# Row terms, output-weight scaling and recurrence products of the first mixer on VectorE, with alpha folded into scales

## The chip, the cores and the metric

The kernel runs on one core of a Trainium2 chip. The metric is the device time of one execution in microseconds; it is the median of three runs. Five engines work side by side, each through its own queue in order: TensorE (PE), VectorE (DVE), ScalarE (ACT), GpSimd (POOL) and SyncE (SP), which here only starts transfers.

## The reference

Two transformer blocks over 512 rows of 1024 numbers in float32. Only the first block is touched:

```python
mod = silu(c) @ w_ada + b_ada
sh_m, sc_m, gt_m, sh_f, sc_f, gt_f = split(mod, 6)        # six modulation rows
u = layer_norm(x) * (1 + sc_m) + sh_m
mix = hybrid_mixer(u, ...)
x = layer_norm(ALPHA * x + (1 + gt_m) * mix, ln1_g, ln1_b)   # ALPHA = 2 ** 0.25
u = layer_norm(x) * (1 + sc_f) + sh_f
ffn = hierarchical_moe(u, ...)                              # 16 experts
x = layer_norm(ALPHA * x + (1 + gt_f) * ffn, ln2_g, ln2_b)

# hybrid_mixer
q, k, v, f_logit, xb, gb = split(u @ w_in)
attn = forgetting_attention(q, k, v, f_logit + b_f)         # 8 heads, causal
xc = causal_conv4(xb) + conv_b                              # rg_lru_branch
a = exp(-8 * sigmoid(gate_r(xc)) * softplus(-lam))
h = scan(h = a * h + sqrt(1 - a * a) * sigmoid(gate_i(xc)) * xc)
lru = h * gelu(gb)
mix = concat(rms_norm(attn, g_attn), rms_norm(lru, g_lru)) @ w_out
```

## The kernel before

Matrix products run in three passes. A weight tile of 128x1024 is loaded (`wraw`), rounded on ScalarE into a high half (`whi`, L275), and the rest is taken on VectorE (`wlo`, L283); L522 to L524 multiply hi by hi, hi by lo and lo by hi. The first mixer fills about the first 323 us of the span. Its weights come in the fixed order xb (4 tiles), gb (4), v (4), q and k in turn (4 each), then eight tiles of the output weight `w_out`. Work for the other engines is written as tasks (generators); between two steps of the projections, each task is advanced by one `yield`. So the place of an operation in an engine's queue follows from how many yields stand before it.

Three tasks are touched. `forget` works out the forget gate. `lru_task` (L988) is the recurrent branch: for two column blocks at a time `conv` (VectorE, L917 and L920) and `gates` (two matmuls, L928, then ScalarE), and after both of them `recur`, with products on VectorE (L945 to L950), one product on GpSimd (L951), the scan on VectorE (L954) and one more product on GpSimd (L958). `ada_rest` (L1195) makes the modulation rows gt_m, sc_f, sh_f, gt_f, in this order: eight tiles of w_ada are loaded by SyncE per row, and tile k, scaled by one column of `cs`, is added to the row. For gt_m this is one VectorE instruction per tile (L1231); for the other three a scaling on ScalarE (L1234) and an add on GpSimd (L1235). `ada_rest` also multiplies the four row tiles of x by ALPHA on GpSimd (L1239).

Before `lru_task` starts, `lru_params` (L1063) works out softplus(-lam) and some halved biases from 4 columns. `times_gt` (L681) multiplies each of the eight output-weight tiles by the row gt_m, on GpSimd, ahead of its split. `mixed` squares a finished column block, adds the squares to those before on GpSimd (L974), and splits the block into halves (L975, L976); `row_scale` turns the sums into 1/rms (L453 to L461), and L1152 adds a product, times that scale, to x. In the attention, one unit's tile runs through the mask (L575), the exponential on ScalarE (L582), reciprocal and scaling (L586, L587), transposes on TensorE (L591) and a copy out of them (L614 or ScalarE's L616).

In the mixture of experts, GpSimd multiplies the four tiles of the new x by ALPHA (L1984, experts 8 to 11).

Of the kernel before, what the change touches and what calls it, by code (L numbers as in the profile page):

```python
# [18 lines left out]
D = 1024  # L19
# [9 lines left out]
RMS_EPS = 1e-6  # L29
ALPHA = 2.0 ** 0.25  # L30
HD = 64
RAWS, PARTS = 5, 4
# [344 lines left out]
class Kern:  # L377
# [303 lines left out]
    def times_gt(self, t, n):  # L681

        assert "gt_m" in self.rows_done
        gt = self.rows["gt_m"][:, None, 512 * n:512 * n + 512]
        self.nc.gpsimd.tensor_tensor(out=t, in0=t, in1=gt.to_broadcast([128, 2, 512]),
                                     op=OP.mult)
# [6 lines left out]
    def first_mixer(self):  # L693
# [10 lines left out]
        for i in range(NT):  # L704
# [11 lines left out]
                               op1=OP.mult)  # L716
        v.tensor_scalar(cs, cs, 0.5, None, op0=OP.mult)


# [178 lines left out]
        xbp, gl, xc, th, tg, ae = {}, {}, {}, {}, {}, {}  # L898
        sp2 = fb.tile([128, 4], F32, name="sp2")
        sp4 = fb.tile([128, 4], F32, name="sp4")  # L900
        brg = fb.tile([128, 4], F32, name="brg")
        big_ = fb.tile([128, 4], F32, name="big")

        def lru_params():
            self.log1p_exp_neg_abs(sp2, self.small("lam", 0, 4), 4)
            nl = self.st(4)
            v.tensor_scalar(nl, self.small("lam", 0, 4), -1.0, 0.0, op0=OP.mult, op1=OP.max)
            v.tensor_tensor(out=sp2, in0=sp2, in1=nl, op=OP.add)
            v.tensor_scalar(sp2, sp2, 2.0, None, op0=OP.mult)
            v.tensor_scalar(sp4, sp2, -2.0, None, op0=OP.mult)  # L910
            v.tensor_scalar(brg, self.small("b_rg", 0, 4), 0.5, None, op0=OP.mult)
            v.tensor_scalar(big_, self.small("b_ig", 0, 4), 0.5, None, op0=OP.mult)

        def conv(m):
# [24 lines left out]
        def recur(m):  # L939


            sq, d = self.g(), self.g()
            t, a, x_c = th.pop(m), ae.pop(m), xc.pop(m)
            nc.scalar.activation(out=sq, in_=t, func=AF.Sqrt, scale=0.25)
            v.scalar_tensor_tensor(out=t, in0=a, scalar=1.0, in1=t, op0=OP.add, op1=OP.mult)  # L945
            v.scalar_tensor_tensor(out=x_c, in0=tg.pop(m), scalar=1.0, in1=x_c,
                                   op0=OP.add, op1=OP.mult)
            yield
            v.scalar_tensor_tensor(out=sq, in0=a, scalar=1.0, in1=sq, op0=OP.add, op1=OP.mult)
            v.tensor_scalar(t, t, -1.0, 1.0, op0=OP.mult, op1=OP.add)  # L950
            nc.gpsimd.tensor_tensor(out=sq, in0=sq, in1=x_c, op=OP.mult)  # L951
            yield
            a = t
            v.tensor_tensor_scan(out=d, data0=a, data1=sq, initial=0.0, op0=OP.mult, op1=OP.add)  # L954
            del a, sq, t, x_c
            while m not in gl:
                yield
            nc.gpsimd.tensor_tensor(out=gl[m], in0=d, in1=gl[m], op=OP.mult)  # L958
            self.dump(f"lruT{m}", gl[m])
            ready.add(("lru", m))  # L960
# [5 lines left out]
        def mixed(nm, m, src, hl):  # L966

            g = self.small(nm, m)
            s2 = self.g()
            nc.scalar.activation(out=s2, in_=src, func=AF.Square)  # L970
            if m == 0:
                ssq[nm] = s2
            else:
                nc.gpsimd.tensor_tensor(out=ssq[nm], in0=ssq[nm], in1=s2, op=OP.add)  # L974
            nc.scalar.activation(out=hl[0][:, m, :], in_=src, func=AF.Copy, scale=g)  # L975
            v.scalar_tensor_tensor(out=hl[1][:, m, :], in0=src, scalar=g,  # L976
                                   in1=hl[0][:, m, :].bitcast(F32), op0=OP.mult,
                                   op1=OP.subtract)

        def row_scale(nm, out):  # L980
            ps = self.psA()
            s2 = ssq.pop(nm)
            for i in range(NT):
                nc.tensor.matmul(ps[:, i:i + 1], lhsT=s2[:, 128 * i:128 * i + 128],
                                 rhs=ones[:, 0:1], start=True, stop=True)
            self.rsqrt(out, ps[:, 0:4], 1.0 / 512, RMS_EPS, 4)

        def lru_task():  # L988
            for pair in range(2):
                for m in (2 * pair, 2 * pair + 1):  # L990
                    while m not in xbp:
                        yield
                    conv(m)
                    yield
                    yield from gates(m)
                    yield
# [65 lines left out]

        lru_params()  # L1063
        ps = self.psA()
# [130 lines left out]
    def ada_rest(self):  # L1195
# [23 lines left out]
        for q, nm in enumerate(names):  # L1219
# [4 lines left out]
            for k in range(KD + 1):  # L1224
                t, nxt = nxt, None
                if k < KD:
                    nxt = self.wp.tile([128, 1024], F32, tag="w", name="ada")
                    nc.sync.dma_start(out=nxt, in_=self.ins["w_ada"][0][
                        128 * k:128 * k + 128, cols[nm]:cols[nm] + 1024])
                if t is not None and q == 0:  # L1230
                    nc.vector.scalar_tensor_tensor(out=a, in0=t, scalar=self.cs[:, k - 1:k],  # L1231
                                                   in1=a, op0=OP.mult, op1=OP.add)
                elif t is not None:
                    nc.scalar.activation(out=t, in_=t, func=AF.Copy, scale=self.cs[:, k - 1:k])  # L1234
                    pool.tensor_tensor(out=a, in0=a, in1=t, op=OP.add)  # L1235
                del t
                if q == 0 and k in (3, 5, 6, 7):
                    i = (3, 5, 6, 7).index(k)
                    pool.tensor_scalar(self.x[:, i, :], self.x[:, i, :], ALPHA, 0.0,  # L1239
                                       op0=OP.mult, op1=OP.add)  # L1240
                yield
                if k == 5 and q > 0:
                    yield from spread(names[q - 1])
# [91 lines left out]
    def first_moe(self):  # L1335
# [25 lines left out]
        def chain(i, dep, pss, before, before_logits):  # L1361
# [54 lines left out]
            g = add("V", 1.2, times(ln1[0]), [d] + before)  # L1416
            r = self.steps_rsqrt(steps, z, q, 1.0 / D, self.eps_ln, -0.5 * LN_EPS)
            m = add("V", 0.3, mean2, [r, g])
# [427 lines left out]
        def places():  # L1846
# [5 lines left out]
            v.reciprocal(out=w1, in_=w1)  # L1852
            v.tensor_tensor(out=w1, in0=w1, in1=gw, op=OP.mult)
            v.tensor_tensor(out=w2, in0=w1, in1=e2, op=OP.mult)
# [103 lines left out]
        for e in range(NE):  # L1958
# [21 lines left out]
            if e == 6:  # L1980
                self.tasks.append(places())
            elif e in (8, 9, 10, 11):
                i = e - 8
                nc.gpsimd.tensor_scalar(x[:, i, :], x[:, i, :], ALPHA, 0.0, op0=OP.mult,  # L1984
                                        op1=OP.add)
            if W.n_dma >= W.limit or e == NE - 1:
# [76 lines left out]
        def tail(i):  # L2063
# [17 lines left out]
            def squares(q, bias):  # L2081
# [14 lines left out]
                op0=OP.add, op1=OP.mult), [d], late=late) for h in range(2)]  # L2096
            r = rsqrt(d, 1.0 / D, self.eps_ln, -0.5 * LN_EPS)
            e = add("A", 0.62, lambda: nc.scalar.activation(
# [984 lines left out]
def kernel(ctx, tc, names, *aps, dbg=None, stop=None):  # L3083
# [24 lines left out]
    k.eps_ln = base.tile([128, 1], F32, name="eps_ln")  # L3108
    nc.vector.memset(k.eps_ln, LN_EPS)
    k.st_first = ExitStack()  # L3110
    k.first = k.pool(k.st_first, "first")
# [106 lines left out]
```

## Time and profile before

| | us |
|---|---|
| median of three runs | 2336.22 (2334.93 to 2337.41) |
| the profiled execution | 2334.09, span 2332.3 |
| TensorE busy in the span | 2201.1 (94%) |
| VectorE busy | 1508.5 (65%) |
| ScalarE busy | 1175.1 (50%) |
| GpSimd busy | 462.2 (20%) |

The page gives each engine's busy time and share of the span, the span in 40 slices, the chain of work that ended last, and groups of instructions with what ended the idle time before them. A timeline lists one engine's instructions by start time, neighbours of one line together, and in brackets how long the engine stood idle before it and which instruction released it.

### The profile page before, as it was taken

Reading aid. Unit: us, or ns where it says so; the run is one execution under the profiler, and the core shown is the slowest. Engines: PE = TensorE matmul, PEld = TensorE weight load, DVE = VectorE, ACT = ScalarE, POOL = GpSimd, SP = SyncE. Lnnn points to the kernel's source line nnn. Section 1 sums busy time; section 2 is a strip of 40 time slices with the busy share of each in tenths; the row PEclk is TensorE's granted clock in tenths of the full one; section 3 lists DMA queues with packets and bytes.
Section 4 is the critical chain, followed back from the end, with each engine's and each line's share of the span. In section 5 each row is a group of like instructions: output and inputs, shape, how many; then the busy total and the mean of one; then the engine's idle time right before and its main releaser. Section 6 shows DMA issues by size and latency. Waiting matters only on the chain.

```text
span 2332.3 us, 30052 instructions
## 1 busy us (share of the span) xinstructions
PE 2201.1 (94%) x10972; PEld 1752.4 (75%) x10972; DVE 1508.5 (65%) x2552; ACT 1175.1 (50%) x2034; POOL 462.2 (20%) x377
## 2 busy tenths in 40 slices
PE   7788786998998799999999999999999999999998
PEld 4566465775565788888888888888888888888887
DVE  7845577979888866656567665257665656666623
ACT  5565444766666666554354443246654435444421
POOL 2465323445544522100000000012310000000000
PEclk9899997999999899999999999999999999999999
DMA  9453227999988433323323333223332332333321
GB/s 301 145 173 117 103 85 254 360 292 311 317 269 273 148 96 90 92 63 109 100 82 100 97 93 118 91 90 91 96 95 60 89 111 84 99 98 100 101 98 64
DMA packets 298092, 323.77 MB, mean 139 GB/s; under 512 B 10976, under 2 KB 216816, under 8 KB 297936
## 3 DMA queue, kind: packets, MB, share of 16 engines
q1 hardware_dynamic: 285904, 281.77, 38.0%
q0 software_dynamic: 12032, 40.00, 5.3%
q8 instruction: 88, 1.44, 0.3%
q14 instruction: 68, 0.56, 0.1%
HBM read 305.15 MB, written 16.52 MB: 138 GB/s over the span
## 4 chain that ended last, share of the span: by engine, by line
PE 71%; DVE 8%; ACT 3%; issue 2%; DMA 1%; POOL 1%; DVEq 0%; ACTq 0%; POOLq 0%
PE ps L523 21%; PE ps L522 21%; PE ps L524 21%; PE ps L2398 2%; DVE wlo L283 2%; PE ps L2561 1%; PE ps L591 1%; PE ps L1331 1%; ACT whi L275 1%; ACT g L2974 1%; PE ps L2680 1%; DVE st L494 1%; PE ps L1443 0%; POOL wlo L283 0%; DVE x L2953 0%
## 5 line engine op out<-in xcount | busy, mean ns | idle before, releaser
L283 DVE TENSOR_TENSOR wlo<-wraw,whi 128x1024 fp32r<-128x1024 f32 (+1 forms) x337 | 433.6, 1290 | 348.0 <-ACT whi L275 181.4
L522 PE MATMUL ps<-hT,whi 128*128 128x512 f32 x1280 | 503.7, 394 | 0.0
L524 PE MATMUL ps<-hT,wlo 128*128 128x512 f32 x1280 | 499.4, 390 | 0.0
L523 PE MATMUL ps<-hT,whi 128*128 128x512 f32 x1280 | 499.1, 390 | 0.0
L275 ACT ACTIVATE whi<-wraw 128x1024 fp32r<-128x1024 f32 (+1 forms) x346 | 360.4, 1048 | 211.4 <-DVE wlo L283 147.4
L524 PEld LDWEIGHTS ps<-hT,wlo 128*128 128x128 f32 x1280 | 240.2, 188 | 51.7
L522 PEld LDWEIGHTS ps<-hT,whi 128*128 128x128 f32 x1280 | 241.0, 188 | 47.3
L523 PEld LDWEIGHTS ps<-hT,whi 128*128 128x128 f32 x1280 | 240.5, 188 | 45.1
L522 PE MATMUL ps<-whi,hi 128*128 128x512 f32 x480 | 189.4, 394 | 0.0
L523 PE MATMUL ps<-wlo,hi 128*128 128x512 f32 x480 | 189.3, 394 | 0.0
L524 PE MATMUL ps<-whi,lo 128*128 128x512 f32 x480 | 189.3, 394 | 0.0
L523 PE MATMUL ps<-wlo,hl 128*128 128x512 f32 (+4 forms) x432 | 175.0, 405 | 9.6 <-DVE wlo L283 6.4
L522 PE MATMUL ps<-whi,hl 128*128 128x512 f32 (+4 forms) x432 | 177.1, 410 | 0.4 <-ACT hl L1638 0.4
L524 PE MATMUL ps<-whi,hl 128*128 128x512 f32 (+4 forms) x432 | 173.4, 401 | 2.6 <-DVE hl L1639 2.6
L283 DVE TENSOR_TENSOR wlo<-wx,whi 128x1024 fp32r<-128x1024 f32 x107 | 147.0, 1396 | 15.2 <-ACT whi L275 13.5
L275 ACT ACTIVATE whi<-wx 128x1024 fp32r<-128x1024 f32 x121 | 125.8, 1058 | 40.4 <-PE ps L523 27.2
L596 ACT ACTIVATE gr<-ps 128x256 fp32r<-128x256 f32 (+2 forms) x128 | 49.1, 384 | 113.8 <-PE ps L591 112.7
L524 PEld LDWEIGHTS ps<-whi,lo 128*128 128x128 f32 x480 | 90.1, 188 | 21.3
L522 PEld LDWEIGHTS ps<-whi,hi 128*128 128x128 f32 x480 | 90.2, 188 | 21.1
L523 PEld LDWEIGHTS ps<-wlo,hi 128*128 128x128 f32 x480 | 90.1, 188 | 21.0
L523 PEld LDWEIGHTS ps<-wlo,hl 128*128 128x128 f32 (+4 forms) x432 | 71.3, 165 | 45.5 <-DVE wlo L283 12.7
L3037 ACT ACTIVATE g<-ps,small 128x512 f32<-128x512 f32 x88 | 68.1, 774 | 61.7 <-PE ps L524 61.7
(506 smaller groups left out, 3994.2 us busy)
## 6 DMA issues: line engine op xcount, KB each, us to landing
wraw<-in_w_in_dram SPq DMA_DIRECT2D x108, 512.0 KB, 3.9
wraw<-in_w_up_dram SPq DMA_DIRECT2D x88, 512.0 KB, 3.8
wx<-in_w_e_down_dram SPq DMA_DIRECT2D x46, 512.0 KB, 4.5
wraw<-in_w_down_dram SPq DMA_DIRECT2D x44, 512.0 KB, 3.6
wx<-in_w_e_gate_dram SPq DMA_DIRECT2D x39, 512.0 KB, 6.3
wx<-in_w_e_up_dram SPq DMA_DIRECT2D x36, 512.0 KB, 7.0
ada<-in_w_ada_dram SPq DMA_DIRECT2D x32, 512.0 KB, 4.6
wraw<-in_w_e_up_dram SPq DMA_DIRECT2D x28, 512.0 KB, 8.4
```

Source lines behind the costliest of these rows:

```text
L275: self.k.nc.scalar.activation(out=hi[:, 0:n_el], in_=t[:, 0:n_el], func=AF.Copy)
L283: eng.tensor_tensor(out=lo[:, 0:n_el], in0=t[:, 0:n_el], in1=hi[:, 0:n_el].bitcast(F32), op=OP.subtract)
L494: p = steps.add("V", 0.13, lambda: v.scalar_tensor_tensor(out=z["q"], in0=z["y"], scalar=z["y"], in1=z["h"], op0=OP.mult, op1=OP.mult), [y ...
L522: mm(ps, lhsT=lhsT[0], rhs=rhs[0], start=first, stop=False)
L523: mm(ps, lhsT=lhsT[0], rhs=rhs[1], start=False, stop=False)
L524: mm(ps, lhsT=lhsT[1], rhs=rhs[0], start=False, stop=last)
L591: nc.tensor.transpose(pt_ps[:, c * 128:(c + 1) * 128], p[:, c * 128:(c + 1) * 128], self.const("ident"))
L596: nc.scalar.activation(out=hi, in_=pt_ps[:, 0:n], func=AF.Copy)
L1331: self.nc.tensor.transpose(pt[:, c * r:(c + 1) * r], src[:, k * 128:(k + 1) * 128], self.ident[0:r, 0:r])
L2398: self.nc.tensor.matmul(ps[q][:, c], lhsT=ws[q][w][:, k, :], rhs=act()[t][k][:, c], start=(j == 0 and k == 0), stop=(j == 2 and k == KD - 1))
L2561: nc.tensor.matmul(ps, lhsT=q, rhs=view(k[part]), start=(part == 0), stop=(part == 1))
L3037: nc.scalar.activation(out=c, in_=ps, func=AF.Identity, scale=w[1], bias=self.small("conv_b2", 44 * l + tile_))
```

## The change

1. `ada_rest`: all four rows are summed on VectorE, one instruction per tile (L1236); ScalarE's 24 scalings and GpSimd's 24 adds are gone. For gt_m a second yield stands behind each tile.
2. `times_gt` (L687), the two products of `recur` (L955, L962) and the adds of `mixed` (L978) go from GpSimd to VectorE.
3. x isn't multiplied by ALPHA any more, neither in the mixer nor in the experts. 1/ALPHA goes into the two scales of `row_scale` and into the router's weight w1 instead, and the epsilon of both normalisations behind is divided by ALPHA squared, so that they return the same.
4. `lru_params` is called at the start of the mixer, ahead of the first normalisation's statistics.
5. `lru_task` yields once more between `conv` and `gates`.

```diff
     def times_gt(self, t, n):
-        self.nc.gpsimd.tensor_tensor(out=t, in0=t, in1=gt.to_broadcast([128, 2, 512]),
+        self.nc.vector.tensor_tensor(out=t, in0=t, in1=gt.to_broadcast([128, 2, 512]),
                                      op=OP.mult)
...
+        def lru_params():
+            self.log1p_exp_neg_abs(sp2, self.small("lam", 0, 4), 4)
...
+        lru_params()
...
         def recur(m):
-            nc.gpsimd.tensor_tensor(out=sq, in0=sq, in1=x_c, op=OP.mult)
+            v.tensor_tensor(out=sq, in0=sq, in1=x_c, op=OP.mult)
...
-            nc.gpsimd.tensor_tensor(out=gl[m], in0=d, in1=gl[m], op=OP.mult)
+            v.tensor_tensor(out=gl[m], in0=d, in1=gl[m], op=OP.mult)
...
-                nc.gpsimd.tensor_tensor(out=ssq[nm], in0=ssq[nm], in1=s2, op=OP.add)
+                v.tensor_tensor(out=ssq[nm], in0=ssq[nm], in1=s2, op=OP.add)
...
-            self.rsqrt(out, ps[:, 0:4], 1.0 / 512, RMS_EPS, 4)
+            self.rsqrt(out, ps[:, 0:4], ALPHA * ALPHA / 512, ALPHA * ALPHA * RMS_EPS, 4)
...
                     conv(m)
                     yield
+                    yield
                     yield from gates(m)
...
-        lru_params()
         ps = self.psA()
...
-                if t is not None and q == 0:
+                if t is not None:
                     nc.vector.scalar_tensor_tensor(out=a, in0=t, scalar=self.cs[:, k - 1:k],
                                                    in1=a, op0=OP.mult, op1=OP.add)
-                elif t is not None:
-                    nc.scalar.activation(out=t, in_=t, func=AF.Copy, scale=self.cs[:, k - 1:k])
-                    pool.tensor_tensor(out=a, in0=a, in1=t, op=OP.add)
                 del t
-                if q == 0 and k in (3, 5, 6, 7):
-                    i = (3, 5, 6, 7).index(k)
-                    pool.tensor_scalar(self.x[:, i, :], self.x[:, i, :], ALPHA, 0.0,
-                                       op0=OP.mult, op1=OP.add)
                 yield
+                if q < 1:
+                    yield
...
-            v.tensor_tensor(out=w1, in0=w1, in1=gw, op=OP.mult)
+            v.scalar_tensor_tensor(out=w1, in0=w1, scalar=1.0 / ALPHA, in1=gw, op0=OP.mult,
+                                   op1=OP.mult)
...
-            elif e in (8, 9, 10, 11):
-                i = e - 8
-                nc.gpsimd.tensor_scalar(x[:, i, :], x[:, i, :], ALPHA, 0.0, op0=OP.mult,
-                                        op1=OP.add)
```

VectorE at the recurrence of the first two column blocks, before: terms of gt_m (L1231), the two products ahead of the scan (L945, L946), a split, two more (L949, L950) and the scan, which the program lists as L954.

```order
L1231 SCALAR_TENSOR_TENSOR gt_m<-ada,cs,gt_m 128x1024 x2
L283 TENSOR_TENSOR wlo<-wraw,whi 128x1024
L1231 SCALAR_TENSOR_TENSOR gt_m<-ada,cs,gt_m 128x1024
L945 SCALAR_TENSOR_TENSOR g<-g 128x512
L946 SCALAR_TENSOR_TENSOR g<-g 128x512
L283 TENSOR_TENSOR wlo<-wraw,whi 128x1024
L949 SCALAR_TENSOR_TENSOR g<-g 128x512
L950 TENSOR_SCALAR g<-g 128x512
L954 SCALAR_TENSOR_TENSOR g<-g 128x512
```

The same place now: the line numbers are shifted by 4, gt_m is L1236, the product that was GpSimd's is L955, the scan L958, and the product with the gelu L962.

```order
L1236 SCALAR_TENSOR_TENSOR gt_m<-ada,cs,gt_m 128x1024
L949 SCALAR_TENSOR_TENSOR g<-g 128x512
L950 SCALAR_TENSOR_TENSOR g<-g 128x512
L285 TENSOR_TENSOR wlo<-wraw,whi 128x1024
L953 SCALAR_TENSOR_TENSOR g<-g 128x512
L954 TENSOR_SCALAR g<-g 128x512
L955 TENSOR_TENSOR g<-g 128x512
L1236 SCALAR_TENSOR_TENSOR gt_m<-ada,cs,gt_m 128x1024
L958 SCALAR_TENSOR_TENSOR g<-g 128x512
L962 TENSOR_TENSOR g<-g 128x512
```

Between the fourth product and the scan there stand one new product and a term of the row, and behind the scan the second new product.

VectorE at the first unit of the attention, before: the last scan, three splits of q and k, then the mask (L575, two rows), reciprocal, scaling.

```order
L954 SCALAR_TENSOR_TENSOR g<-g 128x512
L283 TENSOR_TENSOR wlo<-wraw,whi 128x1024 x3
L575 ISA g,st<-ps,const 128x128
L575 ISA st 128x1
L586 RECIPROCAL st<-st 128x1
L587 TENSOR_SCALAR g<-g,st 128x128
```

The same place now:

```order
L285 TENSOR_TENSOR wlo<-wraw,whi 128x1024
L1236 SCALAR_TENSOR_TENSOR sc_f<-ada,cs,sc_f 128x1024 x3
L285 TENSOR_TENSOR wlo<-wraw,whi 128x1024
L1236 SCALAR_TENSOR_TENSOR sh_f<-ada,cs,sh_f 128x1024 x3
L577 ISA g,st<-ps,const 128x128
L577 ISA st 128x1
L1236 SCALAR_TENSOR_TENSOR sh_f<-ada,cs,sh_f 128x1024
L588 RECIPROCAL st<-st 128x1
L589 TENSOR_SCALAR g<-g,st 128x128
```

Six terms of sc_f and sh_f stand between the last recurrence and the first mask, and a seventh behind the mask, ahead of the reciprocal.

VectorE at the output weights, before: scaling and mask of one unit, two splits, and the first operation of a `row_scale`.

```order
L587 TENSOR_SCALAR g<-g,st 128x384
L575 ISA g,st<-ps,const 128x384
L575 ISA st 128x1
L283 TENSOR_TENSOR wlo<-wraw,whi 128x1024 x2
L453 TENSOR_SCALAR st<-ps 128x4
```

The same place now:

```order
L589 TENSOR_SCALAR g<-g,st 128x384
L577 ISA g,st<-ps,const 128x384
L577 ISA st 128x1
L687 TENSOR_TENSOR wraw<-wraw,gt_m 128x1024
L285 TENSOR_TENSOR wlo<-wraw,whi 128x1024
L687 TENSOR_TENSOR wraw<-wraw,gt_m 128x1024
L285 TENSOR_TENSOR wlo<-wraw,whi 128x1024
L455 TENSOR_SCALAR st<-ps 128x4
```

Each split has the product with gt_m in front of it; three more of these products stand further behind, between the adds to x and the reciprocal of the next unit.

## Rows read from the trace of the kernel before

**Rows 1.** Page: busy time by engine, then the chain that ended last.

```profile
PE 2201.1 (94%) x10972; PEld 1752.4 (75%) x10972; DVE 1508.5 (65%) x2552; ACT 1175.1 (50%) x2034; POOL 462.2 (20%) x377
...
PE 71%; DVE 8%; ACT 3%; issue 2%; DMA 1%; POOL 1%; DVEq 0%; ACTq 0%; POOLq 0%
```

**Rows 2.** What TensorE waited for, 36 to 325 us: total, times, longest.

```profile
PE ps L928 <- DVE g L920: 11.9, 2, 9.1
...
PE ps L591 <- DVE g L587: 6.5, 3, 5.0
...
PE ps L624 <- DVE g L614: 2.9, 2, 1.8
...
PE ps L885 <- issue: 0.9, 1, 0.9
...
PE ps L522 <- DVE st L575: 0.2, 1, 0.2
```

**Rows 3.** TensorE's timeline: start, us, engine, line, operation, [idle before <- releaser].

```profile
74.29 2.84 PE L928 MATMUL ps<-g,bd 128*128 128x512 f32 x4 [2.86 <-DVE g L920]
...
106.72 3.78 PE L928 MATMUL ps<-g,bd 128*128 128x512 f32 x4 [9.09 <-DVE g L920]
...
145.00 0.79 PE L524 MATMUL ps<-uT,wlo 128*128 128x512 f32 x1 [4.29 <-DVE wlo L283]
...
172.68 0.47 PE L591 MATMUL ps<-ident,g 128*128 128x128 f32 x1 [4.95 <-DVE g L587]
...
289.47 2.07 PE L1013 MATMUL ps<-ka,qa 68*128 68x512 f32 x2 [7.72 <-DVE st L453]
```

**Rows 4.** Stretches: busy us of PE, PEld, DVE, ACT, POOL; clock, DMA share, GB/s.

```profile
74.00:172.00 98.00, 80.06 (x302) 60.33 (x302) 55.58 (x46) 59.51 (x70) 52.40 (x25) 0.89 0.48 149
...
108.00:110.00 2.00, 2.00 (x4) 0.73 (x3) 1.94 (x1) 0.69 (x1) 0.86 (x1) 0.50 0.75 220
...
180.00:245.00 65.00, 58.73 (x274) 39.81 (x274) 33.42 (x85) 31.78 (x70) 30.91 (x17) 0.95 0.28 97
```

**Rows 5.** VectorE's timeline, 82 to 148 us.

```profile
82.53 0.69 DVE L946 SCALAR_TENSOR_TENSOR g<-g 128x512 f32<-128x512 f32 x1
83.13 1.22 DVE L283 TENSOR_TENSOR wlo<-wraw,whi 128x1024 fp32r<-128x1024 f32 x1
...
92.12 3.43 DVE L283 TENSOR_TENSOR wlo<-wraw,whi 128x1024 fp32r<-128x1024 f32 x1
...
97.67 3.35 DVE L954 TENSOR_TENSOR_SCAN g<-g 128x512 f32<-128x512 f32 x1 [1.18 <-POOL g L951]
...
147.06 1.23 DVE L954 TENSOR_TENSOR_SCAN g<-g 128x512 f32<-128x512 f32 x1 [1.18 <-POOL g L951]
```

**Rows 6.** GpSimd's timeline at 91 us.

```profile
91.60 2.86 POOL L1235 TENSOR_TENSOR sc_f<-sc_f,ada 128x1024 f32<-128x1024 f32 x1
```

**Rows 7.** VectorE's timeline, 45 to 51 us.

```profile
45.73 0.17 DVE L509 TENSOR_SCALAR g<-g 128x4 f32<-128x4 f32 x1 [0.30 <-ACT g L508]
...
49.84 1.28 DVE L1231 SCALAR_TENSOR_TENSOR gt_m<-ada,cs,gt_m 128x1024 f32<-128x1024 f32 x1
...
51.04 1.22 DVE L283 TENSOR_TENSOR wlo<-wraw,whi 128x1024 fp32r<-128x1024 f32 x1
```

**Rows 8.** Everything that touches the row tiles named ada: waits until a load, landing.

```profile
  DMA ada<-in_w_ada_dram: 16.3, 5
...
DMA to landing us min/median/max: 3.5/4.6/10.0
```

**Rows 9.** VectorE's timeline, 280 to 297 us.

```profile
282.67 6.68 DVE L283 TENSOR_TENSOR wlo<-wraw,whi 128x1024 fp32r<-128x1024 f32 x2 [1.72 <-ACT whi L275]
...
295.94 0.49 DVE L587 TENSOR_SCALAR g<-g,st 128x512 f32<-128x512 f32 x1
```

**Rows 10.** GpSimd's timeline at 583 us.

```profile
583.65 2.85 POOL L1984 TENSOR_SCALAR x<-x 128x1024 f32<-128x1024 f32 x1
```

**Rows 11.** TensorE's timeline at 589 us.

```profile
589.83 0.46 PE L523 MATMUL ps<-wlo,hl 128*80 128x512 f32 x1 [1.98 <-POOL wlo L283]
```

More of the change, by code (lines that the diff above doesn't have):

```diff
@@ L30 @@
 ALPHA = 2.0 ** 0.25
+LN_EPS2 = LN_EPS / ALPHA ** 2
 HD = 64
@@ L717, in first_mixer @@
         v.tensor_scalar(cs, cs, 0.5, None, op0=OP.mult)
+        sp2 = fb.tile([128, 4], F32, name="sp2")
+        sp4 = fb.tile([128, 4], F32, name="sp4")
+        brg = fb.tile([128, 4], F32, name="brg")
+        big_ = fb.tile([128, 4], F32, name="big")
+        def lru_params():
+            self.log1p_exp_neg_abs(sp2, self.small("lam", 0, 4), 4)
+            nl = self.st(4)
+            v.tensor_scalar(nl, self.small("lam", 0, 4), -1.0, 0.0, op0=OP.mult, op1=OP.max)
+            v.tensor_tensor(out=sp2, in0=sp2, in1=nl, op=OP.add)
+            v.tensor_scalar(sp2, sp2, 2.0, None, op0=OP.mult)
+            v.tensor_scalar(sp4, sp2, -2.0, None, op0=OP.mult)
+            v.tensor_scalar(brg, self.small("b_rg", 0, 4), 0.5, None, op0=OP.mult)
+            v.tensor_scalar(big_, self.small("b_ig", 0, 4), 0.5, None, op0=OP.mult)
+        lru_params()
         xnT = [t.rearrange("p (a b) -> p a b", a=2) for t in self.row_tiles(["xnT"] * 4)]
@@ L898, in first_mixer @@
         xbp, gl, xc, th, tg, ae = {}, {}, {}, {}, {}, {}
[L899 to L912, printed above, removed]
         def conv(m):
@@ L1416, in chain @@
             g = add("V", 1.2, times(ln1[0]), [d] + before)
-            r = self.steps_rsqrt(steps, z, q, 1.0 / D, self.eps_ln, -0.5 * LN_EPS)
+            r = self.steps_rsqrt(steps, z, q, 1.0 / D, self.eps_ln2, -0.5 * LN_EPS2)
             m = add("V", 0.3, mean2, [r, g])
@@ L2096, in tail @@
                 op0=OP.add, op1=OP.mult), [d], late=late) for h in range(2)]
-            r = rsqrt(d, 1.0 / D, self.eps_ln, -0.5 * LN_EPS)
+            r = rsqrt(d, 1.0 / D, self.eps_ln2, -0.5 * LN_EPS2)
             e = add("A", 0.62, lambda: nc.scalar.activation(
@@ L3109 @@
     nc.vector.memset(k.eps_ln, LN_EPS)
+    k.eps_ln2 = base.tile([128, 1], F32, name="eps_ln2")
+    nc.vector.memset(k.eps_ln2, LN_EPS2)
     k.st_first = ExitStack()
```

## The prediction

> **What bounds the kernel now.** I read the page first. TensorE is busy for 94% of the span, and the chain that ended last runs through it for 71% and through VectorE for 8% [rows 1]. So a microsecond matters where TensorE stands still. The view of what TensorE waited for between 36 and 325 us, the first mixer, has fourteen lines that add up to 47.3 us; most of them name VectorE [rows 2]. The timeline puts the five longest at 74.29, 106.72, 145.00, 172.68 and 289.47 us: 28.9 us in all [rows 3]. Each costs more than itself: behind the 9.09 us wait the granted clock is 0.50, and over 74 to 172 us it averages 0.89 [rows 4]. 0.11 of 98 us is 10.8 us of full-speed time, part of it in the waits themselves.
>
> Why is VectorE late? Its timeline shows one split of a weight (wlo) taking 1.22 us at 83.13 and the same shape taking 3.43 us at 92.12; one scan takes 1.23 us at 147.06 and another 3.35 us at 97.67 [rows 5]. GpSimd's add of a modulation row starts at 91.60 and takes 2.86 us, across the start of the long split [rows 6]. I read the excess as VectorE being held by a GpSimd operation with two tiles in, and by the same comparison counted about 43 us of excess in 40 to 320 us (an estimate over all VectorE rows there, normal against stretched; the splits and scans quoted are its pattern). The Trainium skill's page "SBUF — State Buffer", section "Who interferes with whom", says that a VectorE instruction with two SBUF inputs and a GpSimd instruction that reads SBUF share an interface, and that the second fully blocks. By that rule the trace agrees: 3.43 less 1.22 is 2.21 us, inside one 2.86 us add.
>
> **The change, part by part.** The sum is made against the profiled execution, 2334.09 us, which is 2.1 us under the median of 2336.22.
>
> Work that moves to VectorE: 24 row terms at 1.28 us busy [rows 7], 1.20 when queued (from the start of the term at 49.84 to that of the split behind it at 51.04), 28.8 us; 8 weights times gt_m, no row on VectorE, taken at the split's 1.22 [rows 5], 9.8 us; 8 recurrence products and 6 sums of squares at the 0.69 of a half-size product [rows 5], 9.7 us. Together 48 us against 43 us of excess that should go: VectorE gets 5 us busier, and gains because the stalls sat where TensorE waited and the new work can sit elsewhere. GpSimd loses all of it, ScalarE 24 scalings.
>
> *Start.* The recurrence's parameters now stand in front of the first normalisation. That chain takes from 45.73 to the row term at 49.84 us [rows 7], 4.1 us; without what I read as a stretch in it, an estimate, 3.4. VectorE is the first engine of the start, so all of it arrives later: +3.4. Bounds: 0, if ScalarE or a load hides it, and 4.1. Gone from 45.7, it lets the forget gate's chain finish sooner, and TensorE's 0.9 us wait in front of L885 goes [rows 2]: −0.9.
>
> *74 to 172 us.* The gates' matmuls stand a step or more behind their convolution, 9 matmuls later at the first place. At 74.29 the convolution is then long done: −2.9, and −1.3 of low clock behind it. The 9.09 us at 106.72 is a convolution queued behind two stretched scans and a stretched split; unstretched and with three terms of 1.2 among them it is ready about when TensorE comes, +0.4 at most: −8.7, and −2.8 of clock. At 145.00 the split waits behind stretched work; I take 0.5 us left of 4.29: −3.8, and −2.6 of clock. The clock terms, 6.7 us, lie under the 10.8 of the window. Together −22.1; bounds −26 and −12, the latter if half of the excess came from something else.
>
> *172.68, the first attention unit.* Here VectorE newly queues four terms of sh_f around the unit's mask and reciprocal. A term needs its load, which takes 3.5 to 10.0 us to land, median 4.6; before, ScalarE bore such waits, 16.3 us in five [rows 8]. All eight loads of a row are issued one by one as terms are consumed, so I expect half of the 4.95 us to stay: −2.3 (0 to −5, and up to +4 if one of the 10 us loads falls there).
>
> *Attention, 180 to 245 us.* VectorE is busy for 33.4 of 65 us, TensorE for 58.7, at a clock of 0.95 [rows 4]. Of the waits for VectorE's g here, about 3 us [rows 2] are stretched copies and scalings (2.9 and, without the 4.95, 1.5 in those two lines, part of it after 245): −2.7. The clock's 0.05 of 65 us is 3.3; I take −2.5. Thirteen new terms of 1.2 us bring VectorE to about 49 less some 11 of excess, 38 of 65; they fit, but some fall between a mask and a reciprocal for which TensorE waits: +2 (0 to +10). Sum −3.2.
>
> *Output weights, 245 to 323 us.* At 289.47 TensorE waits 7.72 us because two splits took 6.68 us [rows 3, 9]. Now each split waits for its own product: 1.2 for the product, about 1.1 on ScalarE, 1.2 for the split, twice: 7.1. This is nearly the same: −1.2. Three more products stand in front of the last units' reciprocal, whose scaling at 295.94 was used at once [rows 9]: +3.5. The eighth weight's product, ScalarE's half and split lie on the path at the end: +2. A product before the first split: +0.6. Gone are the rest of the waits for g, 1.5 [rows 2], and about 1.3 of stretch in the last scale's chain, both estimates: −2.8. Sum +2.1 (−2 to +6).
>
> *Experts.* Four scalings of x leave GpSimd, 2.85 us at 583.65 for one; its split of a weight stood right behind it and TensorE waited 1.98 us for that at 589.83 [rows 10, 11]: −2.0 (0 to −3). The folded constants keep the count of operations.
>
> Sum: +3.4 −0.9 −22.1 −2.3 −3.2 +2.1 −2.0 = −25.0, so 2309; I say **2310 us**.
>
> **The rivals.** *Most of it comes.* If the first unit waits for nothing (another −2.7, −2 of clock), the three products find a gap (−3.5) and the last weight is early (−2), the time is 2299. For it: VectorE has 65 − 38 us free in attention. Against: the queue is in order, and the rows at 295.94 show no gap.
>
> *Terms wait for their loads, slower.* Sixteen terms (sh_f, gt_f) lie among the q, k and attention work on VectorE. In an in-order queue a term whose load is late holds the masks, reciprocals and copies behind it, and TensorE with them. ScalarE's five waits of 16.3 us fell on a queue with slack; on VectorE they would be paid. If each of the sixteen waits w, this costs 16w, so slower begins where w passes 25/16, 1.6 us. With 4.6 us of landing and a step of attention of 65/24, 2.7 us, w would be 1.9 if a load is issued only one step ahead: +30, plus 4 of clock, 2343. Against: the terms are spread one per step, and often a weight's work lies between.
>
> *A saturated VectorE.* Among the rules that speak against the change, the Trainium skill's page "Perfetto Trace Analysis", section "Optimizing Scalar/DVE Operations", says that when VectorE is saturated, moving work to ScalarE or GpSimd can help; the change goes the other way. As a mechanism here: if VectorE set the pace, 48 us less 43 would cost +5 and nothing would be won, and with the start's 3.4 and the products' 5.5 on top 2348. Rows say 33 of 65 busy [rows 4], so it isn't saturated; I give it little.
>
> *Half is given back.* The gain up to 172 comes, but the first unit saves nothing (+2.3), attention turns from −3.2 to +3 because the terms fall in front of reciprocals (+6.2), and the output weights reach their bound (+3.9): 2309 + 12.4 is 2321. For it: both stages queue new work in front of rows that were used at once [rows 9].
>
> **How the numbers follow.** Forecast 0.45, half given back 0.25, most comes 0.15, loads hold VectorE 0.11, saturated 0.04. The range goes from 2297 to 2330: the first unit's and the output weights' bounds below, the second case and its clock above. About 0.2% (4.7 us) is what a measurement can tell from no change. Cases one to three are all faster, with a little of the second near the bound; so faster 0.83, same 0.06, slower 0.11.
>
> **What would show it.** In the profile after: splits and scans of the mixer at 1.2 us throughout; GpSimd nearly idle in 75 to 320; first normalisation 3.4 us later; no TensorE wait over 1 us between 60 and 140, and a clock near 1.00 there; the first transposes of attention near 150 us; the wait at 289 still some 6 us long. It is wrong if VectorE shows waits for the ada loads in its queue with TensorE waiting behind them, or if the splits still take 3.4 us.

## The result, and the profile after

The changed kernel takes 2293.76 us (median of four runs, 2292.26 to 2295.53), the kernel before 2336.81 (2334.93 to 2338.75). The ratio is 0.9814 with a 95% interval of 0.9802 to 0.9825: 43 us, or 1.9%, faster. The forecast was 2310 in a range from 2297 to 2330; the direction was right, the gain is 43 us and not 25, and the time lies 3 us below the range.

The profiled execution of the changed kernel took 2295.53 us (span 2293.8), the longest of its runs; the profiled one of before, 2334.09, lay under the lowest of its timed runs. So the two traces differ by 38.6 us, and only these can be explained from rows. The other 4.5 us are spread between executions.

The page after, its line of busy times (engine, busy us, share, count):

```profile
PE 2191.0 (96%) x10972; PEld 1748.4 (76%) x10972; DVE 1510.5 (66%) x2599; ACT 1147.1 (50%) x2009; POOL 346.8 (15%) x323
```

Against [rows 1], VectorE is busy for 1510.5 us, where it was 1508.5, with 47 instructions more. The work that moved to it is as long as the stretch that went. The groups of VectorE between 40 and 320 us show both, first before, then after (count, busy us, mean ns, idle time in front):

```profile
L283 DVE TENSOR_TENSOR wlo<-wraw,whi 128x1024 fp32r<-128x1024 f32 x28 | 48.9, 1755 | 31.6 <-ACT whi L275 15.2 <-POOL sh_f L1235 11.1 <-issue 3.3
...
L954 DVE TENSOR_TENSOR_SCAN g<-g 128x512 f32<-128x512 f32 x4 | 11.4, 2846 | 4.7 <-POOL g L951 4.7
```

```profile
L285 DVE TENSOR_TENSOR wlo<-wraw,whi 128x1024 fp32r<-128x1024 f32 x29 | 35.3, 1220 | 19.1 <-ACT whi L277 19.0
...
L1236 DVE SCALAR_TENSOR_TENSOR gt_f<-ada,cs,gt_f 128x1024 f32<-128x1024 f32 x8 | 10.2, 1279 | 0.0
...
L687 DVE TENSOR_TENSOR wraw<-wraw,gt_m 128x1024 f32<-128x1024 f32 x8 | 9.6, 1218 | 0.0
L958 DVE TENSOR_TENSOR_SCAN g<-g 128x512 f32<-128x512 f32 x4 | 4.9, 1220 | 0.1
```

Splits fell from a mean of 1755 to 1220 ns, scans from 2846 to 1220, and the moved operations cost what the forecast charged for them, 1279 and 1218 ns. What TensorE still waits for between 36 and 325 us (total, times, longest; a window that now takes in some 40 us of the work behind the mixer) answers to [rows 2]; these are its five largest lines:

```profile
PE ps L1331 <- DVE u L1403: 5.7, 2, 4.8
PE ps L524 <- ACT mix_hl L979: 3.5, 1, 3.5
PE ps L593 <- DVE g L589: 3.3, 2, 2.8
PE ps L525 <- DVE wlo L285: 3.1, 2, 2.0
PE ps L593 <- ACT gt_f L1218: 2.5, 1, 2.5
```

The gates' 11.9 us are gone. TensorE's timeline at the places that answer to [rows 3], and at the two ends of the mixer:

```profile
43.04 0.59 PE L525 MATMUL ps<-uT,wfh 128*8 128x512 f32 x1 [0.42 <-DVE uT L819]
...
148.87 0.47 PE L593 MATMUL ps<-ident,g 128*128 128x128 f32 x1 [2.85 <-DVE g L589]
...
216.75 0.59 PE L524 MATMUL ps<-whi,mix_hl 128*128 128x512 f32 x1 [3.48 <-ACT mix_hl L979]
...
251.46 0.90 PE L593 MATMUL ps<-ident,g 128*128 128x128 f32 x3 [2.55 <-ACT gt_f L1218]
...
279.71 0.79 PE L525 MATMUL ps<-wlo,mix_hl 128*128 128x512 f32 x1 [1.96 <-DVE wlo L285]
```

Taking the same instruction in both traces gives the gain by stage. (In the trace before, the first of these starts at 39.71, the first matmul of the output weights at 247.81, the last split's at 317.81; the first transposes are in [rows 3].)

| stage ends with | before | after | shift so far | gain of the stage | forecast |
|---|---|---|---|---|---|
| forget gate's second matmul | 39.71 | 43.04 | +3.3 | +3.3 | +3.4 |
| first transposes of attention | 172.68 | 148.87 | −23.8 | −27.1 | −25.3 |
| first output-weight matmul | 247.81 | 216.75 | −31.1 | −7.3 | −3.2 |
| last waited-for split | 317.81 | 279.71 | −38.1 | −7.0 | +2.1 |
| end of the span | 2332.3 | 2293.8 | −38.5 | −0.4 | −2.0 |

So the forecast was right within 2 us up to the attention. The attention gave 4 us more, and the output weights 9.

### The profile page after: what moved, and what is told of

It is laid out like the page before. It is cut to its first block, busy times and chain, and to the rows that moved or that the text cites. A ratio compares the mean times of both kernels' runs of the same rounds, so it can differ in the third digit from the quotient of the medians.

```text
span 2293.8 us, 29976 instructions
## 1 busy us (share of the span) xinstructions
PE 2191.0 (96%) x10972; PEld 1748.4 (76%) x10972; DVE 1510.5 (66%) x2599; ACT 1147.1 (50%) x2009; POOL 346.8 (15%) x323
## 4 chain that ended last, share of the span: by engine, by line
PE 60%; DVE 4%; ACT 3%; issue 1%; DMA 1%; POOL 0%; DVEq 0%; ACTq 0%; POOLq 0%
PE ps L524 18%; PE ps L525 18%; PE ps L526 18%; PE ps L2395 2%; PE ps L2558 1%; PE ps L593 1%; DVE wlo L285 1%; ACT g L2971 1%; PE ps L2677 1%; DVE st L496 0%; ACT whi L277 0%; DVE x L2950 0%; DMA g<-in_na_dram 0%; DVE st L2977 0%; DVE hT L3009 0%
## 5 line engine op out<-in xcount | busy, mean ns | idle before, releaser
L285 DVE TENSOR_TENSOR wlo<-wraw,whi 128x1024 fp32r<-128x1024 f32 (+1 forms) x337 | 416.4, 1239 | 333.9 <-ACT whi L277 181.4
```

Source lines behind the costliest of these rows:

```text
L285: eng.tensor_tensor(out=lo[:, 0:n_el], in0=t[:, 0:n_el], in1=hi[:, 0:n_el].bitcast(F32), op=OP.subtract)
```

## Experiments

Theory one, that of the forecast: GpSimd's operations that read tiles stretch VectorE's, TensorE waits for VectorE, and the gain is the stretch that goes. Theory two: the gain comes from the order, with gates further from their convolution, parameters in front, and ScalarE relieved of 24 scalings. All kernels were compared with runs of the kernel before on the same chip, whose median was between 2335.9 and 2337.0. What follows gives differences of medians; against the changed kernel they join different rounds, and taken over the kernel before of the same round they change by up to 0.9 us.

**The rows back on GpSimd.** In the changed kernel:

```diff
-                if t is not None:
+                if t is not None and q == 0:
                     nc.vector.scalar_tensor_tensor(out=a, in0=t, scalar=self.cs[:, k - 1:k],
                                                    in1=a, op0=OP.mult, op1=OP.add)
+                elif t is not None:
+                    nc.scalar.activation(out=t, in_=t, func=AF.Copy, scale=self.cs[:, k - 1:k])
+                    pool.tensor_tensor(out=a, in0=a, in1=t, op=OP.add)
```

> The changed kernel with one part undone: the rows sc_f, sh_f and gt_f are again scaled on ScalarE and added on GpSimd (24 of each). Theory one, GpSimd's operations with two tiles in stretch VectorE: splits and scans between 75 and 250 us are again up to 3.4 us long, TensorE's waits between 70 and 170 us come back in part, and the time is 15 to 25 us above the changed kernel's 2294, some 2312. Theory two, the gain is from the order (gates further from the convolution, parameters in front): the rows matter little, 0 to 5 us, 2294 to 2299.

Measured: 2311.95 us, 18.2 above the changed kernel, as theory one has it. VectorE's timeline at the last recurrence, where the splits and single products are stretched again:

```profile
133.57 2.90 DVE L950 SCALAR_TENSOR_TENSOR g<-g 128x512 f32<-128x512 f32 x1
136.39 2.86 DVE L953 SCALAR_TENSOR_TENSOR g<-g 128x512 f32<-128x512 f32 x1
139.18 2.56 DVE L954 TENSOR_SCALAR g<-g 128x512 f32<-128x512 f32 x1
...
144.23 4.53 DVE L285 TENSOR_TENSOR wlo<-wraw,whi 128x1024 fp32r<-128x1024 f32 x2
```

Three operations of 0.68, 0.68 and 0.42 us take 2.90, 2.86 and 2.56, and the split behind them makes TensorE wait for 7.75 us at 145.51.

**The rows alone.** In the kernel before, the same branch the other way round: all four rows on VectorE, nothing else changed.

```diff
-                if t is not None and q == 0:
+                if t is not None:
                     nc.vector.scalar_tensor_tensor(out=a, in0=t, scalar=self.cs[:, k - 1:k],
                                                    in1=a, op0=OP.mult, op1=OP.add)
-                elif t is not None:
-                    nc.scalar.activation(out=t, in_=t, func=AF.Copy, scale=self.cs[:, k - 1:k])
-                    pool.tensor_tensor(out=a, in0=a, in1=t, op=OP.add)
```

> The kernel before with one part of the change alone: all four rows are summed on VectorE, one instruction per tile, and nothing else is changed. Theory one (stretch): 15 to 25 us faster than before, some 2316. Theory two (order): VectorE gets 29 us of work and no better place for it, so no gain, 2334 to 2342.

Measured: 2323.64 us, 13.4 faster than before. The sign is theory one's, the size a little under what it expected. What probably holds it down: with the recurrence and the weights still on GpSimd, the terms themselves are stretched (a mean of 1669 ns for sc_f, 1281 in the changed kernel).

**GpSimd as busy, but reading nothing.** In the kernel before, with the row adds left out, so that three of the rows hold only their bias:

```diff
-                    pool.tensor_tensor(out=a, in0=a, in1=t, op=OP.add)
+                    pool.memset(t, 0.0)
+                    pool.memset(t, 0.0)
+                    pool.memset(t[:, 0:512], 0.0)
```

> The kernel before in which GpSimd's add of a row tile is replaced by three memsets of the same tile, 2.4 us together, so that GpSimd is as long busy but reads nothing; sc_f, sh_f and gt_f keep only their bias, so this part of the computation is left out. It measures the disputed cost by itself. Theory one (VectorE is held by GpSimd operations that read tiles): splits and scans that run beside the rows are 1.2 us long, and the time is 12 to 25 us under the kernel before. Theory two (what counts is the length and order of the queues): within 4 us of before.

Measured: 2315.22 us, 21.8 faster than before. VectorE got no work, ScalarE kept its 24 scalings, the order is that of before; only the reading went. This separates the two theories most cleanly. In its trace the last waited-for split of the mixer comes 23.0 us earlier (294.85, not 317.81) and the wait at the second gates is 1.94 us (9.09 before); the work behind the mixer, which uses these rows, takes 4.3 us longer, so only the mixer's figure compares like with like. GpSimd's timeline and VectorE's beside it:

```profile
86.45 0.95 POOL L1235 MEMSET ada<- 128x1024 f32 x1
...
140.34 0.95 POOL L1236 MEMSET ada<- 128x1024 f32 x1
141.35 0.53 POOL L1237 MEMSET ada<- 128x512 f32 x1
```

```profile
86.55 1.23 DVE L954 TENSOR_TENSOR_SCAN g<-g 128x512 f32<-128x512 f32 x1 [1.19 <-POOL g L951]
...
141.01 1.23 DVE L283 TENSOR_TENSOR wlo<-wraw,whi 128x1024 fp32r<-128x1024 f32 x1 [5.27 <-ACT whi L275]
...
167.22 1.08 DVE L587 TENSOR_SCALAR g<-g,st 128x384 f32<-128x384 f32 x1
```

A scan that runs beside memsets takes 1.23 us, a split beside two of them 1.23. But a scaling with one tile in (L587) is still held, 1.08 us here where 0.42 is its undisturbed time ([rows 9] have a longer one, of 512 columns, at 0.49).

**The weights' products back on GpSimd.** In the changed kernel:

```diff
-        self.nc.vector.tensor_tensor(out=t, in0=t, in1=gt.to_broadcast([128, 2, 512]),
+        self.nc.gpsimd.tensor_tensor(out=t, in0=t, in1=gt.to_broadcast([128, 2, 512]),
```

> The changed kernel with one part undone: the eight output-weight tiles are again multiplied by gt_m on GpSimd. By the terms of the prediction for the output weights (three products of 3.5 us in front of a reciprocal, 2 at the end, 0.6 in front, all gone; the stretch of 2.8 back) it would be 2 to 4 us faster than the changed kernel, 2290. By the traces of before and after, where this stage became 7 us shorter with the products on VectorE, it is 4 to 8 us slower, some 2300, with splits of 3.4 us near 250 us.

Measured: 2305.33 us, 11.6 above the changed kernel. The forecast's terms for this stage had it faster; they are refuted. Even the 4 to 8 us were too few, mostly because of one instruction. GpSimd's timeline, then VectorE's and TensorE's:

```profile
213.26 6.94 POOL L687 TENSOR_TENSOR wraw<-wraw,gt_m 128x1024 f32<-128x1024 f32 x3
```

```profile
212.85 8.44 DVE L1236 SCALAR_TENSOR_TENSOR gt_f<-ada,cs,gt_f 128x1024 f32<-128x1024 f32 x1
221.22 0.15 DVE L588 RECIPROCAL st<-st 128x1 f32<-128x1 f32 x1
```

```profile
225.17 0.80 PE L524 MATMUL ps<-whi,mix_hl 128*128 128x512 f32 x1 [10.10 <-ACT mix_hl L979]
```

A row term of 1.28 us took 8.44, about as long as its own time and all three products of GpSimd (6.94) one after another. Behind it stands a reciprocal, behind that ScalarE, and TensorE waits for 10.10 us, 6.6 more than at this place in the changed kernel.

**The parameters back.** In the changed kernel:

```diff
-        lru_params()
...
+        lru_params()
         ps = self.psA()
```

> The changed kernel with one part undone: the parameters of the recurrence are worked out at their old place, behind the modulation, not in front of the first normalisation. If the 3.4 us which the prediction charged for the start are paid by the end, it is 3 to 4.5 us faster than the changed kernel, some 2290. Rival: the chain of 3.4 us, back at 47 us, delays the forget gate and the first splits and returns the wait of 0.9 us and more, so that it is within 1.5 us.

Measured: 2291.82 us (2289.30 to 2293.02), 1.9 under the changed kernel, whose runs overlap with these. In its trace the last split is 4.4 us earlier (275.30, not 279.71) and the span 3.9 shorter. That speaks for a start's charge that is paid by the end; but the changed kernel's trace is of its longest run, and the medians' 1.9 us lie under the 3 to 4.5 expected and hardly above the rival's 1.5. How much of the charge reaches the end these runs do not settle. It is the fastest kernel of the study, by less than can be told.

**The gates close behind their convolution.** In the changed kernel:

```diff
                     conv(m)
                     yield
-                    yield
                     yield from gates(m)
```

> The changed kernel with one part undone: one yield, not two, between a convolution and its gates. Theory one says that the wait of 2.86 us at the first gates is one of order and comes back with its low clock, 4 us, the second one of 9 us was stretch and comes back only in part, so 4 to 8 us slower than the changed kernel, some 2300. Theory two (order is the cause of the gain) expects 12 us and more.

Measured: 2297.79 us, 4.0 slower, the lower end of what theory one expected. TensorE's timeline at the two pairs of gates:

```profile
74.97 1.96 PE L932 MATMUL ps<-g,bd 128*128 128x512 f32 x4 [0.78 <-DVE g L924]
...
98.69 2.67 PE L932 MATMUL ps<-g,bd 128*128 128x512 f32 x4 [2.01 <-DVE g L924]
```

The second wait comes back as 2.01 us (9.09 before): most of it was stretch, and the second yield bought the rest. The first comes back as 0.78 us of 2.86, where all of it was expected: it too was mostly not a matter of the order.

**Recurrence and sums back on GpSimd.** In the changed kernel, three products:

```diff
-            v.tensor_tensor(out=sq, in0=sq, in1=x_c, op=OP.mult)
+            nc.gpsimd.tensor_tensor(out=sq, in0=sq, in1=x_c, op=OP.mult)
...
-            v.tensor_tensor(out=gl[m], in0=d, in1=gl[m], op=OP.mult)
+            nc.gpsimd.tensor_tensor(out=gl[m], in0=d, in1=gl[m], op=OP.mult)
...
-                v.tensor_tensor(out=ssq[nm], in0=ssq[nm], in1=s2, op=OP.add)
+                nc.gpsimd.tensor_tensor(out=ssq[nm], in0=ssq[nm], in1=s2, op=OP.add)
```

> The changed kernel with one part undone: the two products of the recurrence and the sums of squares (14 operations of 128x512) are again on GpSimd. Theory one (stretch): each GpSimd operation stretches one VectorE operation by up to 1.2 us, and each scan waits 1.2 us for its product; 2 to 7 us slower than the changed kernel. Theory two: within 1.5 us, because VectorE loses 9.7 us of work and none of it ends a wait.

Measured: 2300.88 us, 7.1 slower, at theory one's upper end. TensorE's wait at the first transposes grows from 2.85 to 5.88 us.

**Alpha folded, alone.** In the kernel before, the third part of the change and nothing else (the two GpSimd scalings of x out, 1/ALPHA in `row_scale` and w1, `eps_ln2`).

> The kernel before with one part of the change alone: x is not multiplied by ALPHA on GpSimd, neither in the mixer nor in the experts, and the constants are folded into the scales. The prediction priced this at 2.0 us (0 to 3), all in the experts: 2334 to 2336. Rival, from the traces of before and after, where the stretch behind the mixer is only 0.4 us shorter although GpSimd's 3.0 us of waits there are gone: the work moves to other waits, within 1 us of before.

Measured: 2329.34 us, 6.6 faster than before; by the traces 3.9. Both sides of what was expected are wrong, and so is the forecast that put all of it in the experts: in the trace 2.9 us are won by 289 us, 3.3 by the end of the mixer, and 0.6 behind it. TensorE's timeline at the two pairs of gates:

```profile
72.74 1.96 PE L930 MATMUL ps<-g,bd 128*128 128x512 f32 x4 [0.67 <-DVE g L922]
106.22 3.38 PE L930 MATMUL ps<-g,bd 128*128 128x512 f32 x4 [11.18 <-DVE g L922]
```

The first wait is 0.67 us where [rows 3] has 2.86, because two terms of gt_m, beside GpSimd's scalings of x before, take 2.58 us and not 5.55. VectorE's and GpSimd's timelines there before:

```profile
64.63 5.55 DVE L1231 SCALAR_TENSOR_TENSOR gt_m<-ada,cs,gt_m 128x1024 f32<-128x1024 f32 x2
```

```profile
65.97 2.08 POOL L1239 TENSOR_SCALAR x<-x 128x1024 f32<-128x1024 f32 x2
...
68.07 1.04 POOL L1239 TENSOR_SCALAR x<-x 128x1024 f32<-128x1024 f32 x1
```

These GpSimd operations have one tile in, so it doesn't take two to hold VectorE. The second wait grows from 9.09 to 11.18 and takes most of the gain back; it shrinks when the row adds go (to 1.94 us with the memsets, 4.48 with the rows alone).

**Rows twice.** In the changed kernel, behind each term of the last two rows:

```diff
                                                    in1=a, op0=OP.mult, op1=OP.add)
+                    if q >= 2:
+                        nc.vector.tensor_tensor(out=a, in0=a, in1=a, op=OP.max)
```

> The changed kernel in which each term of sh_f and gt_f (16, from 140 us on) is followed by a second VectorE operation of the same size (the row's maximum with itself, which changes nothing), 19 us more for VectorE, most of it in the attention. If VectorE has slack there (49 of 73 us busy) and the first sixteen terms cost nothing, these cost under 6 us, below 2300. If VectorE is near the bound, as the rivals of the prediction have it, they cost 12 to 19 us, 2306 to 2313.

Measured: 2308.46 us, 14.7 slower for 19 us more of VectorE. What I expected from slack is wrong, and the side of the rivals (12 to 19 us) came: a second operation behind each of the sixteen terms is paid for at three quarters. The largest piece lies at the first unit of the attention, where the wait of 2.85 us grows by 4.2:

```profile
152.94 0.48 PE L593 MATMUL ps<-ident,g 128*128 128x128 f32 x1 [7.09 <-DVE g L589]
```

Stretches of 149 to 216 us, before, after, and in this kernel (busy us of PE, PEld, DVE, ACT, POOL; clock, DMA share, GB/s):

```profile
149.00:216.00 67.00, 59.88 (x262) 41.88 (x260) 26.18 (x67) 41.07 (x70) 44.58 (x20) 0.94 0.47 156
```

```profile
149.00:216.00 67.00, 63.22 (x296) 42.55 (x296) 44.22 (x111) 31.62 (x76) 2.29 (x3) 0.98 0.46 150
```

```profile
149.00:216.00 67.00, 56.16 (x251) 38.18 (x252) 50.33 (x105) 25.59 (x61) 0.00 (x0) 0.90 0.36 116
```

(The same clock time isn't the same work; in each it lies mostly in the attention.) VectorE goes from 26 to 44 of 67 us while TensorE gets busier, and from 44 to 50 while TensorE loses 7 us and the clock falls to 0.90. VectorE has idle time left there; what costs is work that stands between a mask and its reciprocal.

**Products twice.** In the changed kernel:

```diff
                                      op=OP.mult)
+        self.nc.vector.tensor_tensor(out=t, in0=t, in1=t, op=OP.max)
```

> The changed kernel in which each product of an output weight with gt_m is followed by a second VectorE operation of the same size that changes nothing, 9.7 us more for VectorE. In the trace the three products behind the adds to x cost TensorE 0.4 us of 3.5, so about 3 us of slack lay there and is used up. Then the second three cost their 3.5 in full, the two in front of the splits near 247 us up to 2.4, the last one 1.2: 5 to 7.5 us slower than the changed kernel, some 2300. If there is more slack than that, under 3 us.

Measured: 2303.34 us, 9.6 slower. Two of TensorE's waits:

```profile
255.13 0.90 PE L593 MATMUL ps<-ident,g 128*128 128x128 f32 x3 [5.23 <-ACT gt_f L1219]
...
270.16 0.66 PE L593 MATMUL ps<-ident,g 128*128 128x128 f32 x4 [2.90 <-DVE g L589]
```

The first grew by 2.7 us (two more operations in front of the splits, 2.4), the second by 2.5 (three more in front of the reciprocal, 3.5). In the trace the last split is 9.0 us later, more than expected; the rest, near 3.8, lies in other waits (the one at 216.75 grew from 3.48 to 4.42) and in a lower clock (0.81 over 217 to 255 us, where the changed kernel has 0.89 over 217 to 252), and no run takes it apart.

**Parameters back and gt_m at the old pace.** In the changed kernel, besides the edit of the parameters:

```diff
                 yield
-                if q < 1:
-                    yield
```

> The changed kernel with two parts undone: the parameters of the recurrence at their old place, and one yield, not two, behind each term of gt_m. The first alone gave 1.9 us. If the pace of gt_m matters because its terms stand in VectorE's queue among the first convolutions, the second loses 2 to 4 us and the time is some 2295; if it only brings the later rows forward, away from the attention, it gains 0 to 2 us, 2290 to 2292.

Measured: 2296.89 us, 5.1 above the kernel with the parameters back alone (2.0 by the traces), where 2 to 4 were expected. So the slower pace of gt_m counts: without it TensorE waits 1.34 us at the second gates, 3.25 at 142.44 and 4.67 at 251.28, which are 0 or shorter in the changed kernel.

## Why the prediction was right, and where it was wrong

**The cause: right in the main.** Undone one at a time, the rows cost 18.2 us, the weights' products 11.6, recurrence and sums 7.1 (36.9 together), the second yield 4.0, and the parameters give 1.9. Such parts need not add up, and here they don't: the folded alpha, worth 6.6 alone in the kernel before, and the slower gt_m, worth 5.1, are not among them, and with these the sum passes the 43 us. For the rows, the largest part, the run with memsets shows that what counted was GpSimd's reading, not its length, and not ScalarE's relief, which that run did not have. Theory two has a share: the order, by the second yield and the pace of gt_m, is worth 4.0 and 5.1 us by the medians. VectorE got 2.0 us busier for the 5 forecast.

**Start: right.** +3.3 by the trace, for +3.4. The 0.9 us wait went too, but not for the reason given: it is also gone with the parameters at their old place, in the kernel with alpha folded alone and in the one with the parameters back.

**74 to 172 us: right within 2 us.** The waits at both pairs of gates and at 145 are gone. TensorE was busy for 72.0 of 74 us between 74 and 148, at a clock of 1.00 ([rows 4] have 0.89). Two reasons were off. The wait at the first gates was put down to the order, −2.9; it was mostly stretch (0.78 us came back with one yield, 0.67 was left with the scalings of x gone and the old order). And I charged nothing there for the scalings of x, since I counted GpSimd operations with two tiles in; alone they give 3.3 us in the mixer.

**First unit: right, and for the reason given, terms in the queue.** 2.85 us of the 4.95 stayed, for 2.6 forecast, and doubled terms add 4.2 there. VectorE's timeline shows the queue:

```profile
144.01 1.28 DVE L1236 SCALAR_TENSOR_TENSOR sh_f<-ada,cs,sh_f 128x1024 f32<-128x1024 f32 x1 [0.44 <-DMA ada<-in_w_ada_dram]
145.73 1.28 DVE L1236 SCALAR_TENSOR_TENSOR sh_f<-ada,cs,sh_f 128x1024 f32<-128x1024 f32 x1 [0.43 <-DMA ada<-in_w_ada_dram]
146.93 0.28 DVE L577 CUSTOM_DVE_ANT_0 g<-ps,const 128x128 f32<-128x128 f32 x1
...
147.14 1.28 DVE L1236 SCALAR_TENSOR_TENSOR sh_f<-ada,cs,sh_f 128x1024 f32<-128x1024 f32 x1
148.33 0.16 DVE L588 RECIPROCAL st<-st 128x1 f32<-128x1 f32 x1
```

These two waits, 0.9 us, are all that the whole queue ever waited for an ada load. The rival in which terms wait for their loads, with 1.6 us for each of sixteen as its threshold, didn't come.

**Attention: terms mis-sized.** −7.3 for −3.2. I charged +2 for thirteen terms; no wait of TensorE names them. And I counted 2.7 us of waits as won where TensorE's waits behind the first transposes, up to and with the one at the first output-weight matmul, fell from 9.0 us (0.56, 1.35, 0.25, 1.85, 1.18, 1.39, 2.46) to 4.5 (0.97 and 3.48). Waits that the profile puts down to ScalarE went too. That is not for its 16 scalings fewer there: with the memsets, which keep them, the waits of this stretch are 4.8 us. The one at the first output-weight matmul grew by 1.0, with a term and the product in front of it; the product alone had been charged at +0.6.

**Output weights: the step that failed.** The forecast said +2.1 (−2 to +6), the traces −7.0. The step had three wrong terms, 8.6 of the 9.1 us between them, and all were read from rows without asking who uses the result, and when.

- *The product in front of a reciprocal, +3.5.* I took the scaling at 295.94 as used at once. It works on 512 columns, so its transposes are those that come in fours; the three at 296.51 belong to the 384 columns in front. TensorE's timeline before:

```profile
296.51 0.80 PE L591 MATMUL ps<-ident,g 128*128 128x128 f32 x3
299.42 0.66 PE L591 MATMUL ps<-ident,g 128*128 128x128 f32 x4
```

 The scaling ended at 296.43, its reader started at 299.42: 3.0 us of slack. Afterwards the three products, 3.5 us, left a wait of 0.42. The doubled products then found no slack and cost 2.5 us at that very place.

- *The splits at 289, −1.2.* The length was right, 7.3 us for 7.1. But a duration is no wait: what counts is when the chain starts. VectorE's timeline after:

```profile
244.81 1.22 DVE L687 TENSOR_TENSOR wraw<-wraw,gt_m 128x1024 f32<-128x1024 f32 x1
247.47 1.23 DVE L285 TENSOR_TENSOR wlo<-wraw,whi 128x1024 fp32r<-128x1024 f32 x1 [1.43 <-ACT whi L277]
248.61 1.22 DVE L687 TENSOR_TENSOR wraw<-wraw,gt_m 128x1024 f32<-128x1024 f32 x1
250.95 1.22 DVE L285 TENSOR_TENSOR wlo<-wraw,whi 128x1024 fp32r<-128x1024 f32 x1 [1.12 <-ACT whi L277]
252.09 0.15 DVE L455 TENSOR_SCALAR st<-ps 128x4 f32<-128x4 f32 x1
```

 TensorE starts on the first unit of 512 columns at 245.95 here and at 278.57 before. The second split is over 6.2 us behind that, before (289.35 less 278.57) 10.8: the chain starts earlier against TensorE, the first split 1.5 us behind that start and not 4.1. Before, VectorE was late with the work in front of it, held by five of these products on GpSimd:

```profile
276.08 1.96 DVE L587 TENSOR_SCALAR g<-g,st 128x256 f32<-128x256 f32 x1
...
279.49 0.98 DVE L587 TENSOR_SCALAR g<-g,st 128x384 f32<-128x384 f32 x1
```

```profile
275.05 13.21 POOL L685 TENSOR_TENSOR wraw<-wraw,gt_m 128x1024 f32<-128x1024 f32 x5
```

 Undisturbed, these scalings take 0.35 and 0.42 us. From the start of that unit to the first product with mix_hl behind the next one TensorE took 13.6 us before and 9.0 now: 4.7 won. A wait of some 6 us, the sign that I had named for this place, did not come; it is 2.55.

- *The last weight's product, +2.* It ran at 279.58, beside matmuls; no wait of TensorE on the mixer follows. It cost 0.

**Experts: not settled.** −0.4 for −2.0 in these two traces. GpSimd's 3.0 us of waits there became 0.2, and others came (for a split 1.5 us, for L1543's result 1.7). But the stretch behind the last split differs by more from trace to trace: without the scalings of x it takes 2011.6 to 2014.6 us in the ten traces kept, 1.3 less on average than in the two that have them and are otherwise alike there (before, and the rows alone: 2014.5 and 2014.6). So the term was probably too large, and its size stays open.

**The rivals.** *Most of it comes* was the nearest, 2299, and had been given 0.15 on the strength of the row at 295.94, which was read wrongly. Two of its three conditions came (the products found a gap, the last weight was early), the third, a first unit without a wait, did not; so that it came so near is partly luck. *Half is given back* did not come: neither stage turned. *Saturated* was refuted as a forecast, but the doubled rows show how near it is: another 19 us of VectorE work would have taken a third of the gain back.

## To carry to other kernels

GpSimd's work is not free because GpSimd is idle: take VectorE's duration for one shape beside a reading GpSimd operation and without, and add up the difference before you offload, or to see what bringing work back is worth. For each wait of a sum, find the very instruction that reads the result (its shape tells which) and the place where its chain starts; a row that merely starts soon after is no proof, and a chain of the same length that starts earlier is a gain. Slack found by one move is used up by it, so price a second one by a run.

## What the runs showed of the hardware

A VectorE instruction can be held through several GpSimd operations in a row, not just through the one that runs when it starts: 8.44 us for 1.28 beside three products of 6.94 us together, and before, two terms of gt_m 5.55 us, where 2.58 is their time, beside three scalings in a row. In other places the two engines took turns: with the rows back on GpSimd, three VectorE operations of 2.90, 2.86 and 2.56 us ran beside three adds of 8.22 us together. The Trainium skill's page "SBUF — State Buffer", section "Who interferes with whom", says that in VectorE's two-port modes the engine that issues first has the shared pair for the whole instruction and the other is blocked; the three products behind one another are more than that tells. Which of the engines wins when both are ready, these runs do not tell.

With GpSimd only writing, operations with two tiles in (split, scan) kept their 1.23 us, while a scaling with one tile in was stretched from 0.42 to 1.08. The same section has both cases: an instruction with two SBUF inputs contends with GpSimd's reads and not with its writes alone, and one in a two-port mode, which tensor_scalar can enter, contends with GpSimd. The trace agrees with both times; the mode itself it doesn't show.
